# Second MLP projection of a decoder layer: every fourth block of rows by seven half-block products, MLP in three parts

## The chip, the cores and the metric

The kernel runs on one core of a Trainium2 chip. The metric is the device time of one execution in microseconds (us), the median of several runs.

## What is computed

One decoder layer on 256 tokens of width 2048, all in float32: an RMSNorm, one wide projection, three token mixers (a gated MLP over chunks, a state-space model, stick-breaking attention), their gated sum and an output projection, then an MLP, and a last RMSNorm. The change concerns the MLP alone:

```python
h2 = rmsnorm(x, norm2_g[l])
x = x + jnp.square(jax.nn.relu(h2 @ w_mlp_in[l])) @ w_mlp_out[l]   # (256,2048)@(2048,8192), (256,8192)@(8192,2048)
```

The work is nearly all matrix products. Each float32 operand is split into two parts of a reduced float32 type (`F32R`), `hi` = the rounded value and `lo` = the rest, and a product is the sum of three matmuls: hi by hi, lo by hi and hi by lo.

## The kernel before

All weights are read once from HBM in **units** of 128 partitions by 2 x 512 numbers (512 KB). For the second projection (`w_m2`) a unit is 256 rows by 512 columns; for the first (`w_m1`) 512 rows by 256 columns. A list `plan` names the stages with their units in the order of use. `begin_unit(u, lead)` is called as PE's work on unit u is written: it issues SP's DMA up to unit u + 5 (`dma_to`, four buffers `raw`), splits up to unit u + 3 (`conv_to`: ScalarE casts `raw` to `hi`, line 213, then VectorE subtracts to `lo`, line 214; four buffers each), and then, in `flush`, writes whatever is due: work put off by `later(n, f)` to the n-th next unit. So ScalarE and VectorE do their work in the order of these calls: first the split of a unit three ahead, then evacuations and small work that is due. The engines are scheduled by hand in just that order. In the trace VectorE's operations stand under line 86, a helper.

The activations are kept transposed in pairs of 128 x (2 k-tiles, hi and lo, 256 tokens): `xs2` (tile `xz`) for the MLP's input, `ffs[q]` (tile `ff`) for its hidden layer.

- `run_W` (first projection, lines 272 to 296): per unit eight matmuls of 512 columns (line 288) and eight of 256 (line 292) into one tile `mm` of two PSUM banks; four units make 256 hidden columns. One unit later `wide_sum` adds the halves (ScalarE copy at line 301, VectorE addition), and one unit after that `square` applies the squared ReLU and `split2` splits the result into `ffs`.
- `run_N` (second projection, lines 335 to 357): per unit eight matmuls hi by hi and lo by hi (lines 350, 351), then four with `lo` weights (line 353), 12 of 512 columns, into one tile `mm` whose two banks are the two halves of the tokens. After the last unit of a column group the evacuation is due one unit later: VectorE multiplies by the norm's factor and adds to the residual `x2` (`ev_at` in `do_m2`).

The pool `ps_mm` holds two tiles of two banks, taken in turn, and `ps_sd` four tiles of one bank (`side`). `run_W` and `run_N` use one tile of `ps_mm` per group, so that one is filled while the other is read.

The MLP runs in four parts of 2048 hidden columns: eight groups of the first projection (32 units), then four column groups of 512 of the second (32 units, eight per group), which are added to `x2` part by part. The last group of the last part goes through `run_last`, which shortens the kernel's end.

Of the kernel before, what the change touches and what calls it, by code (L numbers as in the profile page):

```python
# [17 lines left out]
P = 128  # L18
# [73 lines left out]
def hybrid_trunk(  # L92
# [36 lines left out]
    def a4(shape, dt, name):  # L129
        return acts.tile(shape, dt, tag="a4", name=name)  # L130
# [10 lines left out]
        return ps_sd.tile([P, 512], F32, tag="sd", name=name)  # L141


    units = []
# [29 lines left out]
    for q in range(4):  # L174
        for i in range(0, 8, 2):
            if (q, i) == (0, 0):
                ab = [add_units(w_m1, 0, 0, 3), add_units(w_m1, 1, 0, 3)]
                for j in range(2):
                    ab[j] += add_units(w_m1, j, 3, 4)
                plan.append(("m1", (q, i), ab))  # L180
            else:
                plan.append(("m1", (q, i), [add_units(w_m1, 8 * q + i + j, 0, 4) for j in range(2)]))
        for i in range(4):
            plan.append(("m2", (q, i), add_units(w_m2, i, 8 * q, 8 * q + 8)))

    raws, loaded = [], {}

    def dma_to(n, parts=1):
        while len(raws) <= min(n, len(units) - 1):
            u = len(raws)  # L190
            raw = wraw.tile([P, 2, 512], F32, tag="raw", name=f"raw{u}")
# [197 lines left out]
    def sumsq(src, acc, junk):  # L389
        S.activation(junk, src, AF.Square, accum_out=acc)  # L390
# [5 lines left out]
    def split2(dst, i, src):  # L396

        t = dst.pair(i)
        S.copy(t[:, :, 0, :], src)
        V.tensor_sub(t[:, :, 1, :], src, t[:, :, 0, :].bitcast(F32))  # L400
# [678 lines left out]

    def do_m1(q, i0, uss):  # L1080
        if i0 == 0:
            ffs[q] = Split(env, 16, f"ff{q}_")

        def ev(ps, i):
            t = wide_sum(ps, f"relu{q}_{i}")

            def square():
                V.scalar_tensor_tensor(out=t, in0=t, scalar=0.0, in1=t, op0=ALU.max, op1=ALU.mult)
                split2(ffs[q], i, t)

            later(1, square)

        groups = [(us, lambda ps, i=i0 + j: ev(ps, i)) for j, us in enumerate(uss)]
        if (q, i0) == (0, 0):
            run_W(groups, xs2)
        else:
            for g in groups:
                run_W([g], xs2)

    def do_m2(q, c, us):  # L1100
        if q == 3 and c == 0:
            for j in range(2):
                f = a4([P, 2, 512], F32, f"fg{j}")
                S.dma_start(f, final_g[j * 1024:(j + 1) * 1024].rearrange("(a c) -> a c", a=2)
                            .partition_broadcast(P))
                fg.extend((f[:, 0, :], f[:, 1, :]))
            fg.append(a4([P, NT, 512], F32, "last"))

        def ev_at(tt, c0, c1, ps):
            v = x2[c][:, tt, c0:c1]  # L1110
            V.scalar_tensor_tensor(out=v, in0=ps, scalar=st2["rsq"][:, tt:tt + 1], in1=v,
                                   op0=ALU.mult, op1=ALU.add)
            if q == 3:
                part = c + (c0 > 0)
                sumsq(v, ss3[:, tt, part:part + 1], ps)
                V.tensor_mul(v if c < 3 else fg[4][:, tt, c0:c1], v, fg[c][:, c0:c1])
                if c == 3 and c1 == 512:
                    finish(tt)

        if (q, c) == (3, 3):  # L1120
            run_last(us, ffs[q], ev_at)
        else:
            run_N(us, ffs[q], lambda tt, ps: ev_at(tt, 0, 512, ps))


    for kind, arg, us in plan:
        if kind == "s5" and arg == 0:
            x_half(0)
            conv_to(0, parts=2)

            def ev0(b, ps):
                V.tensor_mul(s5x[0][:, 2 * b:2 * b + 2, :], ps, rb)

            def mid0(i):
                if i == 0:
                    x_half(1)
                elif i in (1, 3, 5):
                    x_half(i + 1)
                    conv_to(i + 1)
                    x_half(i + 2)  # L1140
                conv_to(max(i + 1, {4: 6, 5: 7, 6: 8, 7: 10}.get(i, 0)))
                if i in (2, 3, 4, 5):
                    load_x(i - 2)
                if i == 6:
                    spawn("rows", norm1_sums())
                if i == 7:
                    s5_load_b()
                    spawn("s5p", s5_prep(), front=False)

            run_T(us, xs, ev0, lead=0, mid=mid0, delay=8)  # L1150
        elif kind in ("s5", "q", "k", "u"):
            do_proj(kind, arg, us)
        elif kind in ("v", "vg"):
            do_nat(kind, arg, us)
        elif kind.startswith("gate"):
            do_gate(int(kind[4]), arg, us)
        elif kind.startswith("br"):
            do_branch(int(kind[2]), arg, us)
        elif kind == "glu":
            do_glu(arg, us)  # L1160
        elif kind == "out":
            do_out(arg, us)
        elif kind == "m1":
            do_m1(*arg, us)
        else:
            do_m2(*arg, us)

# [19 lines left out]
def _layout(x, norm1_g, w_in, b_gate, gm_norm_g, gm_w_s, gm_b_s, s5_lambda_re, s5_lambda_im, s5_log_dt,  # L1187
# [9 lines left out]
    a["w_glu"] = _tiles(s5_w_glu[0])  # L1197
    a["w_m1"] = _tiles_T(w_mlp_in[0])
    a["w_m2"] = _tiles(w_mlp_out[0])
    a["cols"] = np.concatenate([_cols(norm1_g[0]), _cols(norm2_g[0]), _cols(gm_norm_g[0]),  # L1200
                                _cols(s5_d[0]), _cols(s5_b_glu[0])], axis=1)
    a["b_gate"] = b_gate[0]
# [38 lines left out]
```

## Time and profile before

| | |
|---|---|
| time, median of 3 runs (lowest, highest) | 1542.46 us (1542.14, 1542.51) |
| the profiled execution's own time | 1541.8 us |
| its span from first to last instruction | 1540.0 us |
| PE (TensorE) busy | 1529.7 us, 99% |
| VectorE (DVE) busy | 1097.5 us, 71% |
| ScalarE (ACT) busy | 762.7 us, 50% |
| TensorE's mean granted clock | 0.999 |
| moved by DMA | 298.17 MB, mean 194 GB/s |

A matmul's time in the trace holds the way through the array, so neighbours overlap: the distance from one start to the next says what one costs. PEld is the load of the stationary operand, beside PE. What stands in brackets behind a row is how long the engine was idle before it and what ended that.

### The profile page before, as it was taken

Reading aid. Unit: us, or ns where it says so; the run is one execution under the profiler, and the core shown is the slowest. Engines: PE = TensorE matmul, PEld = TensorE weight load, DVE = VectorE, ACT = ScalarE, POOL = GpSimd, SP = SyncE. Lnnn points to the kernel's source line nnn. Section 1 sums busy time; section 2 is a strip of 40 time slices with the busy share of each in tenths; the row PEclk is TensorE's granted clock in tenths of the full one; section 3 lists DMA queues with packets and bytes.
Section 4 is the critical chain, followed back from the end, with each engine's and each line's share of the span. In section 5 each row is a group of like instructions: output and inputs, shape, how many; then the busy total and the mean of one; then the engine's idle time right before and its main releaser. Section 6 shows DMA issues by size and latency. Waiting matters only on the chain.

```text
span 1540.0 us, 20664 instructions
## 1 busy us (share of the span) xinstructions
PE 1529.7 (99%) x7948; PEld 1300.2 (84%) x7948; DVE 1097.5 (71%) x1456; ACT 762.7 (50%) x948; POOL 12.2 (1%) x21
## 2 busy tenths in 40 slices
PE   9999999999999999999999999999999999999997
PEld 9988888888888887898888888888888888888886
DVE  7886978989999999967655665456545655555554
ACT  7446678455555555564454443344433443344442
POOL 0000000000000000000000000000000000000000
PEclk9999999999999999999999999999999999999999
DMA  9654555555555566656666556555555555555653
GB/s 358 200 190 146 188 185 171 185 196 187 189 197 190 193 197 205 191 179 202 209 205 192 191 180 203 192 191 181 198 193 193 181 192 195 195 184 193 217 192 121
DMA packets 85506, 298.17 MB, mean 194 GB/s; under 512 B 9632, under 2 KB 10656, under 8 KB 85408
## 3 DMA queue, kind: packets, MB, share of 16 engines
q1 hardware_dynamic: 79200, 285.25, 55.9%
q10 hardware_dynamic: 6208, 11.61, 2.3%
q8 instruction: 62, 1.02, 0.3%
q14 instruction: 36, 0.29, 0.1%
HBM read 294.73 MB, written 2.10 MB: 193 GB/s over the span
## 4 chain that ended last, share of the span: by engine, by line
PE 96%; DVE 1%; ACT 1%; issue 1%; DMA 0%; POOL 0%; POOLq 0%; DVEq 0%; ACTq 0%
PE mm L288 20%; PE mm L350 20%; PE mm L351 19%; PE mm L353 19%; PE mm L292 10%; PE mm L320 2%; PE mm L319 2%; PE mm L327 1%; PE pb L642 1%; PE py L742 1%; DVE lo L86 0%; PE pwarm L468 0%; DMA raw<-in_w_m 0%; DVE x L86 0%; ACT hi L213 0%
## 5 line engine op out<-in xcount | busy, mean ns | idle before, releaser
L86 DVE TENSOR_TENSOR lo<-raw,hi 128x1024 fp32r<-128x1024 f32 (+1 forms) x537 | 653.7, 1221 | 377.9 <-ACT hi L213 366.1
L213 ACT CAST hi<-raw 128x1024 fp32r<-128x1024 f32 (+1 forms) x537 | 560.6, 1048 | 610.2 <-PE mm L351 377.6
L288 PE MATMUL mm<-xz,hi 128*128 128x512 f32 x1024 | 256.5, 392 | 0.0
L288 PEld LDWEIGHTS mm<-xz,hi 128*128 128x128 f32 x1024 | 184.4, 189 | 33.2
L350 PE MATMUL mm<-hi,xs 128*128 128x512 f32 x512 | 201.4, 393 | 0.0
L351 PE MATMUL mm<-hi,xs 128*128 128x512 f32 x512 | 199.6, 390 | 0.0
L351 PE MATMUL mm<-hi,ff 128*128 128x512 f32 x480 | 186.8, 389 | 0.0
L350 PE MATMUL mm<-hi,ff 128*128 128x512 f32 x480 | 186.8, 389 | 0.0
L292 PEld LDWEIGHTS mm<-xz,lo 128*128 128x128 f32 x1024 | 139.7, 190 | 10.0
L292 PE MATMUL mm<-xz,lo 128*128 128x256 f32 x1024 | 142.8, 282 | 0.0
L353 PE MATMUL mm<-lo,xs 128*128 128x512 f32 x512 | 136.9, 389 | 0.0
L353 PE MATMUL mm<-lo,ff 128*128 128x512 f32 x480 | 128.3, 389 | 0.0
L350 PEld LDWEIGHTS mm<-hi,xs 128*128 128x128 f32 x512 | 96.1, 188 | 23.5 <-issue 4.1
L353 PEld LDWEIGHTS mm<-lo,xs 128*128 128x128 f32 x512 | 96.1, 188 | 20.2
L351 PEld LDWEIGHTS mm<-hi,xs 128*128 128x128 f32 x512 | 96.2, 188 | 19.4
L353 PEld LDWEIGHTS mm<-lo,ff 128*128 128x128 f32 x480 | 90.1, 188 | 18.7
L351 PEld LDWEIGHTS mm<-hi,ff 128*128 128x128 f32 x480 | 90.1, 188 | 18.6
L350 PEld LDWEIGHTS mm<-hi,ff 128*128 128x128 f32 x480 | 90.1, 188 | 18.6
L288 PE MATMUL mm<-xs,hi 128*128 128x512 f32 x384 | 96.9, 394 | 0.0
L288 PEld LDWEIGHTS mm<-xs,hi 128*128 128x128 f32 x384 | 69.1, 189 | 13.6 <-issue 0.7
L86 DVE TENSOR_TENSOR rt<-bu,cs 128x1024 f32<-128x1024 f32 x64 | 76.6, 1220 | 0.3
L292 PEld LDWEIGHTS mm<-xs,lo 128*128 128x128 f32 x384 | 52.4, 190 | 3.8
(247 smaller groups left out, 1619.7 us busy)
## 6 DMA issues: line engine op xcount, KB each, us to landing
raw<-in_w_m SPq DMA_DIRECT2D x256, 512.0 KB, 4.3
raw<-in_w_in SPq DMA_DIRECT2D x143, 512.0 KB, 4.0
raw<-in_w_wide SPq DMA_DIRECT2D x48, 512.0 KB, 3.9
raw<-in_w_br SPq DMA_DIRECT2D x48, 512.0 KB, 4.2
raw<-in_w_out SPq DMA_DIRECT2D x32, 512.0 KB, 3.7
x<-in_x ACTq DMA_DIRECT2D x8, 512.0 KB, 6.1
raw<-in_w_glu SPq DMA_DIRECT2D x8, 512.0 KB, 4.6
gb<-in_b_gate ACTq DMA_DIRECT2D x12, 256.0 KB, 4.3
```

The lines of the kernel that those rows point to most:

```text
L86: return fn(*a, **kw)
L213: S.copy(hi[:, k, :], raw[:, k, :])
L288: PE.matmul(pt[:, nb, :], lhsT=hi[:, k, nb * P:(nb + 1) * P], rhs=src.both(4 * i + k), start=4 * i + k == 0, stop=False)
L292: PE.matmul(pt[:, nb, T:], lhsT=lo[:, k, nb * P:(nb + 1) * P], rhs=src.hi(4 * i + k), start=False, stop=4 * i + k == last)
L319: PE.matmul(po, lhsT=wh, rhs=src.hi(kt), start=kt == 0 and nb % 2 == 0, stop=False)
L320: PE.matmul(po, lhsT=wh, rhs=src.lo(kt), start=False, stop=False)
L327: PE.matmul(po, lhsT=lo[:, k, nb * P:(nb + 1) * P], rhs=src.hi(kt), start=False, stop=kt == 2 * nk - 1 and nb % 2 == 1)
L350: PE.matmul(ps[tt], lhsT=xh, rhs=hi[:, k, :], start=kt == 0, stop=False)
L351: PE.matmul(ps[tt], lhsT=xl, rhs=hi[:, k, :], start=False, stop=False)
L353: PE.matmul(ps[tt], lhsT=xh, rhs=lo[:, k, :], start=False, stop=kt == 2 * nk - 1)
L642: PE.matmul(pbs[h][i][:, ri * T:(ri + 1) * T], lhsT=s5bs[h // 4][r, h % 4, ri * P:(ri + 1) * P], rhs=s5x[h // 4][r, h % 4, :], start=True, ...
L742: PE.matmul(py[h][32 * i:32 * i + 32, :T], lhsT=cks[h][:, ri, i, :], rhs=s[i // 2][:, ri, i % 2, :], start=ri == 0, stop=ri == 1, tile_pos ...
```

## The change

The MLP is cut into three parts of 12, 12 and 8 blocks of 256 hidden columns. In a part, the second projection goes over two halves of 1024 output columns (`do_m2s`, plan kind `m2s`), except for the last half of the last part, which stays two column groups through `run_N` and `run_last`. In a half, every fourth block (k = 0, 4, 8) is done by Strassen's scheme: the block of 256 rows by 1024 columns is two by two half-blocks of 128 by 512, the tokens are two halves, and seven products of three matmuls stand in for eight. There are 3 + 3 + 2 such blocks over the parts for the first half and 3 + 3 for the second, 14 in all. Such a block counts as three units: `a` and `c` come by DMA from `w_seven` (the same numbers as in `w_m2`, in other pairs), `e` is computed from them. The sums of activations (`form`) are made once per block in `do_m1`.

```diff
+PARTS = (12, 12, 8)
+EVERY = 4
...
+        for h in range(2):
+            if (q, h) == (LAST, 1):
+                for c in (2, 3):
+                    plan.append(("m2", (q, c), add_units(w_m2, c, FIRST[q], FIRST[q + 1])))
+                continue
...
+    def split_unit(u, raw):
...
+        S.copy(hi, raw)
+        V.tensor_sub(lo, raw, hi.bitcast(F32))
+        return hi, lo
...
+        if seven[u] == "a":
+            part["a"] = raw
+            loaded[u] = split_unit(u, raw)
+        elif seven[u] == "c":
+            d = part["d"] = s5w.tile([P, 2, 512], F32, tag="T1", name=f"d{u}", bufs=1)
+            part["x"] = raw
+            V.tensor_sub(d, part["a"], raw[:, 0:1, :].to_broadcast([P, 2, 512]))
+            loaded[u] = split_unit(u, d)
+        else:
+            a, d, x = (part.pop(n) for n in "adx")
+            b = s5w.tile([P, 2, 512], F32R, tag="T2", name=f"b{u}", bufs=1)
+            S.copy(b[:, 0, :], x[:, 1, :])
+            V.tensor_sub(b[:, 1, :], x[:, 1, :], b[:, 0, :].bitcast(F32))
+            V.tensor_add(x[:, 0, :], d[:, 1, :], a[:, 0, :])
+            V.tensor_sub(x[:, 1, :], x[:, 1, :], x[:, 0, :])
+            loaded[u] = (*split_unit(u, x), b)
...
+    def run_seven(us, src, forms, evac):
+        top, bot = two_banks(f"top{us[0][0]}"), two_banks(f"bot{us[0][0]}")
+        bank = {(t, c): p[:, c, :] for t, p in enumerate((top, bot)) for c in range(2)}
+        for n in (1, 5, 7, 6):
+            bank[n] = side(f"p{n}_{us[0][0]}")
...
+        def product(b, x, w):
+            mm(b, x[0], w[0])
+            mm(b, x[1], w[0])
+            mm(b, x[0], w[1])
...
+            if len(u) == 3:
+                a = begin_unit(u[0], 3)
+                product(1, half(2 * k, 0), [w[:, 0, :] for w in a])
+                end_unit()
+                d = begin_unit(u[1], 3)
+                product(5, form(k, 0), [w[:, 0, :] for w in d])
+                product(7, form(k, 2), [w[:, 1, :] for w in d])
+                product((0, 1), form(k, 3), [w[:, 1, :] for w in a])
+                end_unit()
+                hi, lo, b = begin_unit(u[2], 3)
+                product((0, 0), half(2 * k + 1, 0), (b[:, 0, :], b[:, 1, :]))
+                product(6, form(k, 1), (hi[:, 0, :], lo[:, 0, :]))
+                product((1, 0), half(2 * k + 1, 1), (hi[:, 1, :], lo[:, 1, :]))
+                if k == shared:
+                    later(1, lambda: evac[0](bank))
+                end_unit()
+            elif k < len(us) - 1:
+                for c in range(2):
+                    w = begin_unit(u[c], 3)
+                    for t in range(NT):
+                        std(u[c], k, c, t, w)
+                    end_unit()
+            else:
+                w0 = begin_unit(u[0], 3)
+                std(u[0], k, 0, 0, w0)
+                end_unit()
+                w1 = begin_unit(u[1], 2)
+                std(u[1], k, 1, 0, w1)
+                std(u[0], k, 0, 1, w0)
+                std(u[1], k, 1, 1, w1)
+                later(1, lambda: evac[1](top, bot))
+                end_unit()
...
+        def ev_shared(bank):
+            p1, p12 = r[0][:, 0, :], r[0][:, 1, :]
+            p21, p22 = r[1][:, 0, :], r[1][:, 1, :]
+            S.copy(p1, bank[1])
+            S.copy(p12, bank[5])
+            V.tensor_add(p21, bank[6], p1)
+            V.tensor_add(p12, p12, p21)
+            V.tensor_add(p22, bank[7], p12)
+            V.tensor_add(p21, bank[7], p21)
+        def ev(top, bot):
+            V.tensor_add(r[0], top, r[0])
+            V.tensor_add(r[1], bot, r[1])
+            for t in range(NT):
+                for c in range(2):
+                    later(1 + t, lambda t=t, c=c: add_m2(q, 2 * h + c, t, 0, 512, r[t][:, c, :]))
```

`std` is the plain product of one unit for one half of the tokens: four matmuls with `hi`, then two with `lo`. The tiles `top` and `bot` are the two tiles of `ps_mm`: the sums of the upper and of the lower half of the tokens for all 1024 columns, filled through the whole half. Four products that go into more than one sum have the four `side` banks (`p`), read by `ev_shared` after the last Strassen block.

Three places of the order on VectorE follow. The first is the **end of a part**, where the second projection ends and the next part's first begins. Before (the evacuation of the last column group is the row `x_3<-mm`):

```order
L86 TENSOR_TENSOR lo_8864<-raw_8825,hi_8863 128x1024
L86 TENSOR_TENSOR lo_8882<-raw_8843,hi_8881 128x1024
L86 TENSOR_TENSOR lo_8901<-raw_8861,hi_8900 128x1024
L86 SCALAR_TENSOR_TENSOR x_3_7337<-mm_8750,rsq,x_3_7337 128x512 x2
L86 TENSOR_TENSOR lo_8925<-raw_8879,hi_8924 128x1024
L86 TENSOR_TENSOR lo_8947<-raw_8898,hi_8946 128x1024
```

Now:

```order
L91 TENSOR_TENSOR lo_9665<-raw_9611,hi_9664 128x1024
L91 TENSOR_TENSOR lo_9669<-raw_9629,hi_9668 128x1024
L91 TENSOR_TENSOR m2r_9185<-top_9187,m2r_9185 128x1024
L91 TENSOR_TENSOR m2r_9186<-bot_9188,m2r_9186 128x1024
L91 TENSOR_TENSOR lo_9693<-raw_9641,hi_9692 128x1024
L91 SCALAR_TENSOR_TENSOR x_2_7164<-m2r_9185,rsq,x_2_7164 128x512
L91 SCALAR_TENSOR_TENSOR x_3_7337<-m2r_9185,rsq,x_3_7337 128x512
```

Behind the splits of the two units that the next stage needs third and fourth stand two additions of 1024 columns, which read `top` and `bot`; the work on `x2` comes later and reads their results. PE's next group there takes the tile of `top`.

The second is the **change of halves** inside a part. Before, at the change from the second column group to the third:

```order
L86 TENSOR_TENSOR lo_8588<-raw_8549,hi_8587 128x1024
L86 TENSOR_TENSOR lo_8607<-raw_8567,hi_8606 128x1024
L86 SCALAR_TENSOR_TENSOR x_1_6991<-mm_8456,rsq,x_1_6991 128x512 x2
L86 TENSOR_TENSOR lo_8627<-raw_8585,hi_8626 128x1024
L86 TENSOR_TENSOR lo_8645<-raw_8604,hi_8644 128x1024
```

Now, from the first half to the second, from the split of unit `a` on:

```order
L91 TENSOR_TENSOR lo_9136<-raw_9099,hi_9135 128x1024
L91 TENSOR_TENSOR d_9153<-raw_9099,raw_9117 128x1024
L91 TENSOR_TENSOR lo_9156<-d_9153,hi_9155 128x1024
L91 TENSOR_TENSOR b_9195<-raw_9117,b_9195 128x512
L91 TENSOR_TENSOR raw_9117<-d_9153,raw_9099 128x512
L91 TENSOR_TENSOR raw_9117<-raw_9117 128x512
L91 TENSOR_TENSOR lo_9201<-raw_9117,hi_9200 128x1024
L91 TENSOR_TENSOR lo_9205<-raw_9151,hi_9204 128x1024
L91 TENSOR_TENSOR m2r_8717<-top_8719,m2r_8717 128x1024
L91 TENSOR_TENSOR m2r_8718<-bot_8720,m2r_8718 128x1024
```

The difference `d`, its split, three half-size steps for `b` and the sums, and the split of `e` now stand ahead of the additions that read `top` and `bot`.

The third is the **start of the first half** of a part, after the last group of the first projection. Before (`relu_7<-mm` evacuates that group):

```order
L86 TENSOR_TENSOR lo_8263<-raw_8209,hi_8262 128x1024
L86 TENSOR_TENSOR lo_8285<-raw_8234,hi_8284 128x1024
L86 TENSOR_TENSOR lo_8308<-raw_8260,hi_8307 128x1024
L86 TENSOR_TENSOR relu_7_8311<-mm_8208,relu_7_8311 128x512
L86 TENSOR_TENSOR lo_8329<-raw_8282,hi_8328 128x1024
L86 SCALAR_TENSOR_TENSOR relu_7_8311<-relu_7_8311 128x512
L86 TENSOR_TENSOR ff_7_8333<-relu_7_8311,ff_7_8333 128x2x256
```

Now, from the split of unit `a` on (`relu_11<-mm` evacuates that group):

```order
L91 TENSOR_TENSOR lo_8643<-raw_8594,hi_8642 128x1024
L91 SCALAR_TENSOR_TENSOR relu_10_8623<-relu_10_8623 128x512
L91 TENSOR_TENSOR ff_10_8647<-relu_10_8623,ff_10_8647 128x2x256
L91 TENSOR_TENSOR d_8668<-raw_8594,raw_8617 128x1024
L91 TENSOR_TENSOR lo_8671<-d_8668,hi_8670 128x1024
L91 TENSOR_TENSOR b_8692<-raw_8617,b_8692 128x512
L91 TENSOR_TENSOR raw_8617<-d_8668,raw_8594 128x512
L91 TENSOR_TENSOR raw_8617<-raw_8617 128x512
L91 TENSOR_TENSOR lo_8698<-raw_8617,hi_8697 128x1024
L91 TENSOR_TENSOR lo_8728<-raw_8666,hi_8727 128x1024
L91 TENSOR_TENSOR relu_11_8731<-mm_8616,relu_11_8731 128x512
```

The addition that reads the last group's tile stands behind the same unit's split as before, but a Strassen block's whole preparation is now ahead of it.

## Rows read from the trace of the kernel before

**Rows 1.** The page: busy time of each engine; the clock TensorE was granted, 40 slices.

```profile
PE 1529.7 (99%) x7948; PEld 1300.2 (84%) x7948; DVE 1097.5 (71%) x1456; ACT 762.7 (50%) x948; POOL 12.2 (1%) x21
...
PEclk9999999999999999999999999999999999999999
```

**Rows 2.** The page: the chain that ended last, shares of the span by line.

```profile
PE mm L288 20%; PE mm L350 20%; PE mm L351 19%; PE mm L353 19%; PE mm L292 10%; PE mm L320 2%; PE mm L319 2%; PE mm L327 1%; PE pb L642 1%; PE py L742 1%; DVE lo L86 0%; PE pwarm L468 0%; DMA raw<-in_w_m 0%; DVE x L86 0%; ACT hi L213 0%
```

**Rows 3.** Timeline, end of the second part: start, us, engine, line, out<-in, [idle before<-releaser].

```profile
1172.61 0.39 PE L350 MATMUL mm<-hi,ff 128*128 128x512 f32 x1
...
1175.33 0.39 PE L350 MATMUL mm<-hi,ff 128*128 128x512 f32 x1
...
1177.14 1.07 PE L353 MATMUL mm<-lo,ff 128*128 128x512 f32 x4
1177.34 1.05 ACT L213 CAST hi<-raw 128x1024 fp32r<-128x1024 f32 x1 [1.67 <-PE mm L351]
...
1178.05 1.98 PE L288 MATMUL mm<-xz,hi 128*128 128x512 f32 x8
1178.42 1.23 DVE L86 TENSOR_TENSOR lo<-raw,hi 128x1024 fp32r<-128x1024 f32 x1 [1.50 <-ACT hi L213]
```

**Rows 4.** Groups of VectorE by shape: line, operation, tiles, shapes, count, busy us, mean ns.

```profile
L86 DVE TENSOR_TENSOR lo<-raw,hi 128x1024 fp32r<-128x1024 f32 x535 | 652.3, 1223 | 377.3 <-ACT hi L213 365.5 <-PE mt L408 6.0 <-PE zt L408 4.5
...
L86 DVE TENSOR_TENSOR ff<-relu,ff 128x512 fp32r<-128x512 f32 x32 | 22.2, 693 | 22.0 <-ACT ff L399 22.0
L86 DVE SCALAR_TENSOR_TENSOR relu<-relu 128x512 f32<-128x512 f32 x32 | 21.9, 685 | 0.0
L86 DVE TENSOR_TENSOR relu<-mm,relu 128x512 f32<-128x512 f32 x32 | 21.9, 684 | 0.0
L86 DVE SCALAR_TENSOR_TENSOR x<-mm,rsq,x 128x512 f32<-128x512 f32 x30 | 21.3, 744 | 0.0
```

**Rows 5.** Groups of ScalarE by shape.

```profile
L213 ACT CAST hi<-raw 128x1024 fp32r<-128x1024 f32 x535 | 559.3, 1050 | 609.7 <-PE mm L351 377.6 <-PE mm L288 119.9 <-issue 71.5
...
L399 ACT CAST ff<-relu 128x512 fp32r<-128x512 f32 x32 | 19.8, 619 | 60.9 <-DVE relu L86 60.9
```

**Rows 6.** Timeline where the second part turns from first to second projection.

```profile
1088.18 2.00 PE L288 MATMUL mm<-xz,hi 128*128 128x512 f32 x8
...
1090.27 1.05 ACT L213 CAST hi<-raw 128x1024 fp32r<-128x1024 f32 x1 [1.75 <-PE mm L288]
...
1090.98 0.40 PE L350 MATMUL mm<-hi,ff 128*128 128x512 f32 x1
...
1091.22 0.58 ACT L301 COPY relu<-mm 128x512 f32<-128x512 f32 x1
1091.35 1.23 DVE L86 TENSOR_TENSOR lo<-raw,hi 128x1024 fp32r<-128x1024 f32 x1 [1.57 <-ACT hi L213]
...
1092.49 0.68 DVE L86 TENSOR_TENSOR relu<-mm,relu 128x512 f32<-128x512 f32 x1
```

**Rows 7.** DMA issues: queue, count, KB each, median us from issue to landing.

```profile
raw<-in_w_m SPq DMA_DIRECT2D x256, 512.0 KB, 4.3
```

**Rows 8.** Windows at the kernel's end: busy time (x instructions), then PEclk, DMA share, GB/s.

```profile
1530.00:1532.00 2.00, 1.69 (x15) 1.49 (x13) 0.27 (x1) 0.00 (x0) 0.00 (x0) 1.00 0.00 0
...
1534.00:1536.00 2.00, 0.00 (x0) 0.00 (x0) 1.29 (x4) 0.00 (x0) 0.00 (x0) 1.00 0.53 196
1536.00:1538.00 2.00, 0.00 (x0) 0.00 (x0) 0.00 (x0) 0.00 (x0) 0.00 (x0) 0.61 0.99 311
```

**Rows 9.** Timeline of PE, first weight unit.

```profile
6.75 0.41 PE L319 MATMUL mm<-xs,hi 128*128 128x256 f32 x1
...
7.18 0.32 PE L319 MATMUL mm<-xs,hi 128*128 128x256 f32 x1
...
7.95 0.28 PE L319 MATMUL mm<-xs,hi 128*128 128x256 f32 x1
...
8.19 0.28 PE L319 MATMUL mm<-xs,hi 128*128 128x256 f32 x1
```

More of the change, by code (lines that the diff above doesn't have):

```diff
@@ L35 @@
 MAGIC = 12582912.0
+PARTS = (12, 12, 8)
+FIRST = [sum(PARTS[:q]) for q in range(len(PARTS) + 1)]
+LAST = len(PARTS) - 1
+EVERY = 4
 C_G1, C_G2, C_GM, C_D, C_GLU = 0, 16, 32, 40, 48
@@ L141, in side @@
         return ps_sd.tile([P, 512], F32, tag="sd", name=name)
-    units = []
+    units, seven = [], {}
     def add_units(src, g, k0, k1):
@@ L173, in hybrid_trunk @@
         plan.append(("out", i, add_units(w_out, i, 0, 8)))
-    for q in range(4):
-        for i in range(0, 8, 2):
+    for q, nk in enumerate(PARTS):
+        for i in range(0, nk, 2):
+            g = FIRST[q] + i
             if (q, i) == (0, 0):
@@ L181, in hybrid_trunk @@
             else:
-                plan.append(("m1", (q, i), [add_units(w_m1, 8 * q + i + j, 0, 4) for j in range(2)]))
-        for i in range(4):
-            plan.append(("m2", (q, i), add_units(w_m2, i, 8 * q, 8 * q + 8)))
+                plan.append(("m1", (q, i), [add_units(w_m1, g + j, 0, 4) for j in range(2)]))
+        for h in range(2):
[3 more added lines that the diff above has]
+                continue
+            us = []
+            for k in range(nk):
+                ku = FIRST[q] + k
+                if k % EVERY == 0:
+                    n = len(units)
+                    units.extend((w_seven[h, ku // EVERY, 0], w_seven[h, ku // EVERY, 1], None))
+                    seven.update({n: "a", n + 1: "c", n + 2: "e"})
+                    us.append((n, n + 1, n + 2))
+                else:
+                    us.append([add_units(w_m2, 2 * h + c, ku, ku + 1)[0] for c in range(2)])
+            plan.append(("m2s", (q, h), us))
     raws, loaded = [], {}
@@ L190, in dma_to @@
             u = len(raws)
+            if units[u] is None:
+                raws.append(None)
+                continue
             raw = wraw.tile([P, 2, 512], F32, tag="raw", name=f"raw{u}")
@@ L204, in conv_to @@
             raws[u] = None
+            if u in seven:
+                conv_seven(u, raw)
+                nconv[0] += 1
+                continue
             if u >= len(units) - 4:
@@ L216, in conv_to, with conv_seven @@
             nconv[0] += 1
+    part = {}
+    def split_unit(u, raw):
+        hi = whi.tile([P, 2, 512], F32R, tag="hi", name=f"hi{u}")
+        lo = wlo.tile([P, 2, 512], F32R, tag="lo", name=f"lo{u}")
+        S.copy(hi, raw)
+        V.tensor_sub(lo, raw, hi.bitcast(F32))
+        return hi, lo
+    def conv_seven(u, raw):
+        if seven[u] == "a":
[14 more added lines that the diff above has]
+            loaded[u] = (*split_unit(u, x), b)
     BAR = "bar"
@@ L358, in run_N, with mm, half, form @@
             end_unit()
+    def run_seven(us, src, forms, evac):
[3 more added lines that the diff above has]
+            bank[n] = side(f"p{n}_{us[0][0]}")
+        triples = sum(len(u) == 3 for u in us)
+        left = {b: 6 * (len(us) - triples) for b in bank if b not in (1, 5, 6, 7)}
+        for b in (1, 5, 6, 7, (0, 0), (0, 1), (1, 0)):
+            left[b] = left.get(b, 0) + 3 * triples
+        begun = set()
+        def mm(b, x, w):
+            left[b] -= 1
+            PE.matmul(bank[b], lhsT=x, rhs=w, start=b not in begun, stop=left[b] == 0)
+            begun.add(b)
+        def half(kt, t):
+            return tuple(x[:, t * P:(t + 1) * P] for x in (src.hi(kt), src.lo(kt)))
+        def form(k, f):
+            return tuple(forms[k][:, f, e, :] for e in range(2))
+        def product(b, x, w):
+            mm(b, x[0], w[0])
+            mm(b, x[1], w[0])
+            mm(b, x[0], w[1])
+        def std(u, k, c, t, w):
+            for part in range(2):
+                for e in range(2):
+                    xh, xl = half(2 * k + e, t)
+                    if part == 0:
+                        mm((t, c), xh, w[0][:, e, :])
+                        mm((t, c), xl, w[0][:, e, :])
+                    else:
+                        mm((t, c), xh, w[1][:, e, :])
+        shared = max(k for k, u in enumerate(us) if len(u) == 3)
+        for k, u in enumerate(us):
+            if len(u) == 3:
[20 more added lines that the diff above has]
+                    end_unit()
+            else:
+                w0 = begin_unit(u[0], 3)
[7 more added lines that the diff above has]
+                end_unit()
+        assert not any(left.values())
@@ L1089, in square, with sums @@
                 split2(ffs[q], i, t)
+                if i % EVERY == 0:
+                    later(1, sums)
+            def sums():
+                f = s5w.tile([P, 4, P], F32, tag="gb", name=f"sums{q}_{i}", bufs=1)
+                V.scalar_tensor_tensor(out=f[:, 0, :], in0=t[:, 0, P:], scalar=-1.0, in1=t[:, 1, P:],
+                                       op0=ALU.mult, op1=ALU.subtract)
+                V.scalar_tensor_tensor(out=f[:, 1, :], in0=f[:, 0, :], scalar=-1.0, in1=t[:, 0, :P],
+                                       op0=ALU.mult, op1=ALU.subtract)
+                V.tensor_sub(f[:, 2, :], t[:, 0, :P], t[:, 0, P:])
+                V.tensor_sub(f[:, 3, :], t[:, 1, :P], f[:, 1, :])
+                fs = forms[q][i] = a4([P, 4, 2, P], F32R, f"form{q}_{i}")
+                S.copy(fs[:, :, 0, :], f)
+                V.tensor_sub(fs[:, :, 1, :], f, fs[:, :, 0, :].bitcast(F32))
             later(1, square)
@@ L1098, in do_m1, with load_fg @@
                 run_W([g], xs2)
-    def do_m2(q, c, us):
[L1101 to L1121, printed above, removed]
-        else:
-            run_N(us, ffs[q], lambda tt, ps: ev_at(tt, 0, 512, ps))
+    def load_fg():
+        for j in range(2):
+            f = a4([P, 2, 512], F32, f"fg{j}")
+            S.dma_start(f, final_g[j * 1024:(j + 1) * 1024].rearrange("(a c) -> a c", a=2)
+                        .partition_broadcast(P))
+            fg.extend((f[:, 0, :], f[:, 1, :]))
+        fg.append(a4([P, NT, 512], F32, "last"))
@@ new lines, in add_m2 @@
+    def add_m2(q, c, tt, c0, c1, ps):
+        v = x2[c][:, tt, c0:c1]
+        V.scalar_tensor_tensor(out=v, in0=ps, scalar=st2["rsq"][:, tt:tt + 1], in1=v,
+                               op0=ALU.mult, op1=ALU.add)
+        if q == LAST:
+            n = c + (c0 > 0)
+            sumsq(v, ss3[:, tt, n:n + 1], ps)
+            V.tensor_mul(v if c < 3 else fg[4][:, tt, c0:c1], v, fg[c][:, c0:c1])
+            if c == 3 and c1 == 512:
+                finish(tt)
+    def do_m2(q, c, us):
+        if c == 3:
+            run_last(us, ffs[q], lambda tt, c0, c1, ps: add_m2(q, c, tt, c0, c1, ps))
+        else:
+            run_N(us, ffs[q], lambda tt, ps: add_m2(q, c, tt, 0, 512, ps))
@@ new lines, in do_m2s @@
+    def do_m2s(q, h, us):
+        if q == LAST:
+            load_fg()
+        r = [a4([P, 2, 512], F32, f"m2r{q}{h}{t}") for t in range(NT)]
+        def ev_shared(bank):
[13 more added lines that the diff above has]
+                    later(1 + t, lambda t=t, c=c: add_m2(q, 2 * h + c, t, 0, 512, r[t][:, c, :]))
+        run_seven(us, ffs[q], forms[q], (ev_shared, ev))
@@ L1164, in hybrid_trunk @@
             do_m1(*arg, us)
+        elif kind == "m2s":
+            do_m2s(*arg, us)
         else:
@@ L1199, in _layout @@
     a["w_m2"] = _tiles(w_mlp_out[0])
+    b = a["w_m2"].reshape(2, 2, -1, P, 2, 512)[:, :, ::EVERY]
+    a["w_seven"] = np.stack([np.stack([b[:, r, :, :, 0], b[:, 1 - r, :, :, 1]], axis=3) for r in range(2)],
+                            axis=2)
     a["cols"] = np.concatenate([_cols(norm1_g[0]), _cols(norm2_g[0]), _cols(gm_norm_g[0]),
```

6 lines of the change are left out of this document (4 added, 2 removed).

## Prediction

> **What bounds the kernel now.** I read the page's busy times first: PE is busy 99% of the span, at a granted clock of 9 tenths or more in all 40 slices [rows 1]. The chain that ended last says the same of the path: its large shares are all matmul lines, and VectorE's and ScalarE's lines have 0% each [rows 2]. So a matmul removed is time gained, and a wait put on PE is time lost, one for one. VectorE (71%) and ScalarE (50%) have room on average.
>
> The price of a matmul is read from the timeline: two units of the second projection start 2.72 us apart, at 1172.61 and 1175.33 [rows 3], and hold 12 matmuls of 512 columns, so one costs 2.72 / 12 = 0.227 us. A unit of the first projection takes 1090.98 - 1088.18 = 2.80 us [rows 6].
>
> The same timelines show how stages follow each other now. At the end of a part the next matmul starts at 1178.05, one matmul's distance behind the last [rows 3]; where the first projection turns into the second PE goes on at 1090.98 while the tile just filled is emptied by ScalarE at 1091.22 and by VectorE at 1092.49 [rows 6]. PE waits at neither, since it goes on in the other tile of its pool. These places are what the change alters.
>
> **The change part by part.** *Matmuls.* A Strassen block needs 7 x 3 = 21 matmuls where two units need 24. With 14 blocks, 42 matmuls go: 42 x 0.227 = **9.5 us gained**. Order of the sums, fewer parts and the doubled width add or remove none.
>
> *Work on VectorE and ScalarE.* Per block VectorE has four steps of 1024 columns (the splits of a, c and e, and d) at 1.22 us and three of 512 at 0.69 [rows 4]: 7.0 us, where two units have 2.4. PE needs 21 x 0.227 = 4.8 us for the block, so VectorE falls behind inside it, but four blocks of rows together cost VectorE 7.0 + 6 x 1.22 = 14.3 us against 4.8 + 6 x 2.72 = 21.1 us of PE. With splits three units ahead I cost this at nothing inside a half; its cover is the plain units ahead of the block, whose splits take half of their time. The sums in `do_m1` (four steps of 128 columns, each under the 0.69 of 512, one of 512, and a cast of 0.62 [rows 5]) fit into a group of 4 x 2.80 = 11.2 us, in which VectorE has 4 x 1.22 + 3 x 0.69 = 7.0. The two DMAs of a block carry the same 512 KB each as two units' did. A raw buffer is held a little longer, and one DMA takes 4.3 us to land [rows 7], which lies within the three units' lead: nothing.
>
> *New waits.* `run_seven` takes both tiles of `ps_mm` and fills them to the end of a half. So whatever comes next has no free tile, and PE waits for VectorE where it did not. There are eight such places. I work each out with t = 0 where PE would start the next stage, and with three habits of the rows: a matmul ends 0.39 us after its start; a cast starts 0.04 us after the end of the last matmul that reads the old `hi` (which started one matmul before 1177.14, so it ended at 1177.30, and the cast starts at 1177.34); a subtraction starts 0.03 us after its cast [rows 3].
>
> (1) *End of a part, into the next part's first group, and in the last part into its third column group: three times.* The last unit's `hi` is read up to the third matmul from the end: it starts at -0.68 and ends at -0.29. The cast that takes this buffer runs from -0.25 to 0.80 (1.05 us [rows 5]), its subtraction from 0.82 to 2.05, and only then the addition that empties `top`. It has 1024 columns and no row of its own. From below, a subtraction of 1024 from the other memory takes 1.22; from above, two additions of 512 out of PSUM take 2 x 0.68 = 1.37 [rows 4]. I take 1.22, since for 512 columns the two memories differ by 0.01. So `top` is free at 3.25 and PE starts at about **3.3 us**. At best the addition goes ahead of one split (2.1); at worst PE needs `bot` too, one addition later (4.5).
>
> (2) *First half to second half, twice.* PE has nine matmuls in the `side` banks first, 9 x 0.227 = 2.04 us, then needs `top`. VectorE's queue up to `top` is the block's whole preparation: from the cast of a (its buffer is read until -8.45, three units ahead) cast 1.05, split 1.22, d 1.22, cast 1.05, split 1.22, three half steps 2.07, cast 1.05, split 1.22, the next unit's split 1.22, addition 1.22. That is 12.5 us and 0.2 of gaps from -8.42: `top` is free at 4.25, a wait of **2.2 us**. If the preparation were no bound, the splits at the end would still give some 3.0 - 2.04, 1.0; if it is later by a DMA or a cast, 3.5.
>
> (3) *First projection to first half, three times.* `top` is long free; `bot` holds the last group of the first projection and is needed after 18 matmuls, at 4.08. The queue starts with the cast of a at -9.09, three units of 2.80 and the 0.71 us by which a cast leads a unit [rows 6]: cast 1.05, split 1.22, the group's square 0.69, cast 0.62, subtraction 0.69, then as in (2) from d to the next unit's split 9.05, and the addition that empties `bot`, 0.68. The sum is 14.0 us, so `bot` is free at 4.9. The wait is **0.9 us**, between 0 and 2.
>
> *Sum.* Waits 3 x 3.3 + 2 x 2.2 + 3 x 0.9 = 17.0 us (8 to 26 with the ends above), gain 9.5: the profiled execution goes from 1541.8 to 1549.3. The median of the runs lies 0.66 above that execution, so I forecast **1550.0 us**, 7.5 us or 0.5% slower, and 1541 to 1559 with the bounds.
>
> *The clock.* In the windows of the kernel's end PE's last matmul is over at 1531.7, the granted clock is still 1.00 until 1536 and 0.61 from there to 1538 [rows 8]; with levels of 2.4 and 1.2 GHz, 0.61 is 0.44 us at the upper and the rest at the lower, so the fall came after some 4.7 us of rest. My longest wait is 3.3, so I let the clock stay. The Trainium skill's page "TensorE: Matmul & The Clock Gate", section "HAM oscillation", warns of just such waits between bursts of matmuls, after each of which the array is back at half its clock; the rows of the end bear out the fall, but after a longer rest, and by it the sum would be that of the second rival.
>
> **The rivals.** *The banks come free in time* (faster). If VectorE reads each tile before PE needs it, only the 42 matmuls are left: 1542.5 - 9.5 = 1533.0. It decides where the eight waits sum to under 9.5 - 3.1 = 6.4 us, under 0.8 each. For it: VectorE idles much of the second projection [rows 1, 4], and today's changes of stage cost PE nothing [rows 3, 6]. Against: the additions can't start before the last matmul of a half, two splits stand ahead of them, and no third tile exists. Chance 0.08.
>
> *The clock falls at the long waits* (slower still). The first weight unit shows what that costs: two matmuls of 256 columns take 7.18 - 6.75 = 0.43 us early and 8.19 - 7.95 = 0.24 soon after [rows 9]. PE's work had begun at about 1 us, so some 6 us at half pace lose about 3 us. One to three falls give 1553 to 1559. For it: three waits over 3 us. Against: the rows of the end, 4.7 us. Chance 0.12.
>
> *Only the ends of parts cost.* If the block's preparation runs ahead, the five waits of (2) and (3) fall under 0.5 us each: 9.9 + 2.5 - 9.5 = 2.9 at most and 0.4 at least, so 1543 to 1545. What counts is whether d and the half steps are done before the half ends; they wait for no matmul, but for the split of a, which does. Chance 0.13.
>
> *VectorE becomes the bound at each block*: if the lead is used up, each of 14 blocks loses up to 7.0 - 4.8 = 2.2 us, 31 in all; half of that gives 1565. Against: 14.3 of 21.1 us. Chance 0.04.
>
> *The change doesn't do what it says*: the order on PE has 42 fewer matmuls of 512 columns, so I leave that out.
>
> **How the numbers follow.** The forecast has 0.63. Its own bounds reach 1541 to 1559, most of it 1545 to 1555. The range that holds eight in ten leaves out the fast rival, the blocks as a bound, and two or three falls of the clock: 1542 to 1557. A measurement of this kernel can tell 0.2%, 3.1 us, from no change. Faster by more than that: the fast rival and a tail of the third, 0.09. Within it (1539.4 to 1545.5): most of the third rival and the forecast's low end, 0.15. Slower: the rest, 0.76.
>
> **What would show it.** Right: PE's waits on the addition that reads `top`, at three ends of parts, near 3 us each, and on `top` near 2 us at two changes of halves; 42 fewer matmuls at an unchanged 0.227; the clock at 1.00. The first column of the waits would name `m2r` as what `mm` and `top` waited for. Wrong: no PE waits of over 1 us in the MLP (the fast rival), a clock under 1.00 in slices of the MLP (the second), or waits on `hi` and `lo` inside the halves (the fourth).

## The result: 15.8 us slower, where 7.5 were forecast

The changed kernel took 1558.26 us (1557.83 to 1560.14) against 1542.45: a ratio of 1.0105, 95% interval 1.0088 to 1.0123. Slower was right, the size was not: the time lies 1.3 us above the range. The profiled execution took 1557.83 us.

The page of the changed kernel, busy times and granted clock, answers to [rows 1]:

```profile
PE 1529.2 (98%) x7906; PEld 1295.7 (83%) x7906; DVE 1183.3 (76%) x1588; ACT 790.8 (51%) x994; POOL 12.2 (1%) x21
...
PEclk9999999999999999999999999999999999999999
```

PE is busy as long as before, though 42 matmuls fewer stand in the span, which is 16 us longer. The clock's digits are 9 as before, since slices of 39 us average over what follows; its mean over the span is 0.993 where it was 0.999. The list of PE's waits, those in the MLP (us in total, times, longest), where before had none ([rows 3, 6] show two of the places):

```profile
PE mm L345 <- DVE m2r L91: 6.3, 2, 3.2
PE top L433 <- DVE m2r L91: 4.0, 2, 2.0
PE mm L407 <- DVE m2r L91: 3.2, 1, 3.2
PE bot L433 <- DVE relu L91: 1.8, 3, 0.6
```

These are the eight places of the forecast: three ends of parts (2 + 1), two changes of halves, three starts of a first half. The timeline of the first end of a part, where the second projection ran into the first without a wait before [rows 3]:

```profile
1090.84 2.58 DVE L91 TENSOR_TENSOR lo<-raw,hi 128x1024 fp32r<-128x1024 f32 x2 [2.86 <-ACT hi L241]
1090.91 0.61 PE L433 MATMUL bot<-lo,ff 128*128 128x512 f32 x2
...
1093.33 1.22 DVE L91 TENSOR_TENSOR m2r<-top,m2r 128x1024 f32<-128x1024 f32 x1
1094.47 1.22 DVE L91 TENSOR_TENSOR m2r<-bot,m2r 128x1024 f32<-128x1024 f32 x1
...
1094.70 3.75 PE L345 MATMUL mm<-xz,hi 128*128 128x512 f32 x8 [3.17 <-DVE m2r L91]
...
1098.25 1.91 PE L349 MATMUL mm<-xz,lo 128*128 128x256 f32 x8
...
1099.95 2.20 PE L345 MATMUL mm<-xz,hi 128*128 128x512 f32 x8
...
1102.94 1.32 PE L345 MATMUL mm<-xz,hi 128*128 128x512 f32 x5
```

The queue is the one worked out: two splits end at 1093.42, the addition that empties `top` runs behind them, and PE starts 0.15 us after it. From the last start before (1090.91 and one matmul, 1091.14) to 1094.70 are 3.56 us, 3.3 more than a matmul's 0.227. But then the next group's unit takes 1099.95 - 1094.70 = 5.25 us, where it took 2.80 [rows 6], and the one behind it 1102.94 - 1099.95 = 2.99. The windows (busy times, then the granted clock) say why:

```profile
1092.00:1094.00 2.00, 0.00 (x0) 0.00 (x0) 1.88 (x3) 0.16 (x1) 0.00 (x0) 0.88 0.46 117
1094.00:1096.00 2.00, 1.30 (x3) 1.14 (x4) 1.68 (x2) 0.00 (x0) 0.00 (x0) 0.50 0.84 266
...
1098.00:1100.00 2.00, 2.00 (x11) 1.90 (x10) 0.00 (x0) 1.04 (x1) 0.00 (x0) 0.50 0.00 0
1100.00:1102.00 2.00, 2.00 (x10) 1.61 (x10) 1.75 (x2) 0.00 (x0) 0.00 (x0) 0.92 0.00 0
```

The clock fell inside PE's rest, at about 1093.5 (0.88 over 2 us is 0.48 us at half of the full clock), and came back at about 1100.3 (0.92). The third end of a part shows the same:

```profile
1500.64 0.77 PE L407 MATMUL mm<-hi,ff 128*128 128x512 f32 x1 [3.17 <-DVE m2r L91]
...
1508.95 0.39 PE L407 MATMUL mm<-hi,ff 128*128 128x512 f32 x1
```

Two units, 24 matmuls, lie between these starts: 8.31 us where 2 x 2.72 = 5.44 are the rule.

The timeline of the first change of halves:

```profile
1025.98 0.39 PE L433 MATMUL p<-lo,form 128*128 128x512 f32 x1
...
1027.02 1.22 DVE L91 TENSOR_TENSOR m2r<-top,m2r 128x1024 f32<-128x1024 f32 x1
...
1028.38 0.94 PE L433 MATMUL top<-hi,form 128*128 128x512 f32 x2 [2.01 <-DVE m2r L91]
...
1032.80 1.08 PE L433 MATMUL top<-hi,ff 128*128 128x512 f32 x4
```

and the windows there, with a shorter fall:

```profile
1026.00:1028.00 2.00, 0.37 (x2) 0.00 (x0) 2.00 (x2) 1.04 (x1) 0.00 (x0) 1.00 0.53 131
1028.00:1030.00 2.00, 1.62 (x5) 1.30 (x6) 2.00 (x3) 0.64 (x1) 0.00 (x0) 0.66 0.90 279
1030.00:1032.00 2.00, 2.00 (x6) 1.61 (x5) 2.00 (x4) 0.41 (x1) 0.00 (x0) 0.50 0.56 199
1032.00:1034.00 2.00, 2.00 (x10) 1.57 (x10) 2.00 (x3) 1.05 (x1) 0.00 (x0) 0.98 0.51 195
```

Here PE rested from 1026.4 to 1028.38, and the clock fell after PE had begun again, at about 1028.6, for some 3.4 us: the first 12 matmuls took 1032.80 - 1028.38 = 4.42 us where 2.72 are the rule. The second change of halves has a rest of the same 2.01 us, and the second end of a part one of 3.17, and neither is followed by a fall. Behind the second change the 12 matmuls take 1302.80 - 1299.94 = 2.86 us with the clock at 1.00, and the rows of that end show a unit at nearly its usual pace, 1367.56 - 1364.70 = 2.86 us:

```profile
1364.70 2.06 PE L345 MATMUL mm<-xz,hi 128*128 128x512 f32 x8 [3.17 <-DVE m2r L91]
...
1367.56 1.78 PE L345 MATMUL mm<-xz,hi 128*128 128x512 f32 x7
```

The timeline at the start of a first half, with the third kind of wait:

```profile
963.77 0.39 PE L433 MATMUL p<-lo,form 128*128 128x512 f32 x1
964.01 0.68 DVE L91 TENSOR_TENSOR relu<-mm,relu 128x512 f32<-128x512 f32 x1
...
964.75 0.74 PE L433 MATMUL bot<-hi,ff 128*128 128x512 f32 x2 [0.59 <-DVE relu L91]
```

The group of the new additions out of PSUM (count, ns min/median/max):

```profile
L91 DVE TENSOR_TENSOR m2r<-top,m2r x5: 1215/1217/1218, 1027.0 to 1499.3; 128x1024 f32<-128x1024 f32 x5
```

The addition of 1024 columns takes 1.217 us; I had taken 1.22 between 1.22 and 1.37.

### The profile page after: what moved, and what is told of

It is laid out like the page before. It is cut to its first block, busy times and chain, and to the rows that moved or that the text cites. A ratio compares the mean times of both kernels' runs of the same rounds, so it can differ in the third digit from the quotient of the medians.

```text
span 1556.1 us, 20790 instructions
## 1 busy us (share of the span) xinstructions
PE 1529.2 (98%) x7906; PEld 1295.7 (83%) x7906; DVE 1183.3 (76%) x1588; ACT 790.8 (51%) x994; POOL 12.2 (1%) x21
## 5 line engine op out<-in xcount | busy, mean ns | idle before, releaser
L241 ACT CAST hi<-raw 128x1024 fp32r<-128x1024 f32 (+1 forms) x509 | 530.0, 1049 | 486.6 <-PE mm L408 216.0
L349 PEld LDWEIGHTS mm<-xz,lo 128*128 128x128 f32 x1024 | 140.5, 191 | 10.1
L433 PE MATMUL bot<-hi,ff 128*128 128x512 f32 x364 | 98.9, 390 | 1.8 <-DVE relu L91 1.8
L433 PE MATMUL top<-hi,ff 128*128 128x512 f32 x336 | 89.9, 389 | 0.0
L433 PEld LDWEIGHTS bot<-hi,ff 128*128 128x128 f32 x364 | 68.2, 188 | 17.3 <-DVE relu L91 3.1
L433 PEld LDWEIGHTS top<-hi,ff 128*128 128x128 f32 x336 | 63.1, 188 | 13.3
L251 ACT CAST hi<-raw 128x1024 fp32r<-128x1024 f32 x28 | 29.5, 1052 | 60.0 <-DVE raw L91 38.9
L433 PE MATMUL bot<-lo,ff 128*128 128x512 f32 x182 | 57.2, 389 | 0.0
```

Source lines behind the costliest of these rows:

```text
L251: S.copy(hi, raw)
L349: PE.matmul(pt[:, nb, T:], lhsT=lo[:, k, nb * P:(nb + 1) * P], rhs=src.hi(4 * i + k), start=False, stop=4 * i + k == last)
L433: PE.matmul(bank[b], lhsT=x, rhs=w, start=b not in begun, stop=left[b] == 0)
```

## The experiments

All are edits of the changed kernel. Two theories stood after the result: **(T)** the eight waits as forecast, and on top some 8 us of matmuls at half the clock, which the waits bring about; **(R)** the remainder is work that the change adds or delays (VectorE's load, the new form of matmul, the longer parts).

**e_fill: PE kept busy in the waits.** The fills write a bank that no one reads afterwards.

```diff
+        def fill(po, n):
+            for i in range(n):
+                PE.matmul(po, lhsT=src.hi(0)[:, 0:P], rhs=src.both(0), start=True, stop=True)
...
+                if k == 0:
+                    fill(bank[6], fills[0])
                 product((0, 1), form(k, 3), [w[:, 1, :] for w in a])
...
+        if fills[2]:
+            fill(side(f"fill{us[0][0]}"), fills[2])
...
```

> The changed kernel with matmuls of no use put where PE waits: nine before the first product into top at each change of halves, three before product 6 at the start of a first half, fourteen at each end of a part; each 512 columns, 0.227 us, into a bank that is not read afterwards. They fit into the waits measured in the changed kernel (starts 2.40, 0.98 and 3.57 us apart where 0.227 is the rule, so 2.2, 0.75 and 3.3 us), so by themselves they move nothing. Theory (some 8 us of the change's cost are matmuls at half the clock after the waits): PE has no rest, the granted clock stays at 1.00 to the last matmul, and the time falls from 1558.3 to about 1550. Rival (the remainder is something else, such as slower matmuls in the new form or work of VectorE that is late): the time stays at 1558, or rises by what the fills overrun.

Measured: 1551.04 us, ratio to before 1.0057 (1.0040 to 1.0074). The windows around the first end of a part:

```profile
1090.00:1092.00 2.00, 2.00 (x10) 1.67 (x9) 1.87 (x3) 0.55 (x1) 0.00 (x0) 1.00 0.29 66
1092.00:1094.00 2.00, 1.99 (x9) 1.37 (x8) 2.00 (x2) 0.00 (x0) 0.00 (x0) 1.00 0.84 270
1094.00:1096.00 2.00, 2.00 (x15) 1.78 (x14) 0.08 (x1) 0.78 (x1) 0.00 (x0) 1.00 0.50 193
```

With the waits still there, but no rest, the clock stays at 1.00 (0.999 over the span, as before the change) and 7.2 us come back by the medians, 6.7 between the profiled executions. That is the price of the falls, and it is not VectorE's: its work is the same (1184.2 us busy against 1183.3). 1.7 us above 1542.2 - 9.5 + 16.6 are left: 0.6 lie ahead of the MLP, whose first matmul starts at 824.88 instead of 824.31, and 1.1 inside the halves, where e_early_relu has them too.

**e_early: the waits taken away where both tiles are read too late.** `top` is complete 2.7 us before `bot`; it is now read then.

```diff
                 std(u[1], k, 1, 0, w1)
+                evac[1](0, top)
                 std(u[0], k, 0, 1, w0)
+                conv_to(u[1] + 3)
                 std(u[1], k, 1, 1, w1)
-                later(1, lambda: evac[1](top, bot))
+                evac[1](1, bot)
...
```

> The changed kernel, but top is read as soon as its last matmul is written, ahead of the next unit's split, while PE still fills bot for 2.7 us; bot is read ahead of the last split. Theory (PE waits for the tiles of ps_mm alone): the waits at three ends of parts go from 3.3 us to none, at two changes of halves from 2.2 to about 0.3, at three starts of a first half they stay at 0.75; the clock stays at 1.00. 1542.5 - 9.5 + 0.6 + 2.3 = 1535.9 us. Rival (VectorE's load is the bound and the waits only show it): waits of the same sum turn up at the splits of the block that is prepared at the change of halves, and the time stays over 1545.

Measured: 1536.47 us, ratio 0.9962 (0.9947 to 0.9977). In the list of PE's waits one group of the MLP is left:

```profile
PE bot L433 <- DVE relu L91: 1.8, 3, 0.6
```

Five waits go, and the clock's mean is back at 0.999. VectorE is busy as long as before, 1183.6 us, so its load was not behind them. What turns up elsewhere is small, and the forecast had it (0.3 at each change of halves): the next block there waits for the addition that reads `bot`, as the next run's rows show.

**e_early_relu: the third kind of wait too.** In the first unit of a half what is due is written ahead of the split.

```diff
+        if due_first:
+            flush()
         conv_to(u + lead)
...
+                a = begin_unit(u[0], 3, due_first=k == 0)
```

> As e_early, and at the start of a first half the last group of the first projection is read ahead of the split of the unit three ahead. Theory: the three waits of 0.75 us go too, since that addition then ends at about 3.8 us and PE needs the tile at 4.1: 1533.6 us, all of the 42 matmuls' 9.5 us but 0.6. Rival: the split that now comes later is what PE waits for next, 0.5 us or more each, and the time is that of e_early.

Measured: 1533.96 us, ratio 0.9946 (0.9931 to 0.9961), faster than both kernels. PE's waits of the whole profile, none in the MLP:

```profile
PE pwarm L605 <- POOL ones L588: 1.0, 1, 1.0
PE pyc L999 <- ACT le L991: 0.9, 1, 0.9
```

Against the 1532.7 that 42 matmuls alone would give, 1.3 us are missing. Most of them lie inside the halves. The first two take 1086.23 - 959.24 = 126.99 us; at the same place e_parts, with plain units alone, has 576 matmuls in 1090.42 - 959.83 = 130.59, so 18 fewer would take 126.5. The same reckoning gives 0.5 for the second pair of halves and 0.1 for the last half: 1.1 us in all. About 0.5 of it is a wait that the list of PE's waits leaves out, since the load of the weights has it:

```profile
1026.86 0.30 PEld L435 LDWEIGHTS bot<-hi,ff 128*128 128x128 f32 x2 [0.40 <-DVE m2r L91]
```

It delays PE by 0.24 us at each of the two changes of halves. The other 0.6 are spread over the 14 blocks, some 0.04 us in each; their cause is open. So (R) has a small share: 1.1 us, and it stays with the waits taken away.

**e_parts: the cut into parts alone** (second projection by `run_N` in all parts, no halves, no Strassen blocks):

```diff
-            if (q, h) == (LAST, 1):
-                for c in (2, 3):
+            if True:
+                for c in (2 * h, 2 * h + 1):
                     plan.append(("m2", (q, c), add_units(w_m2, c, FIRST[q], FIRST[q + 1])))
...
-                if i % EVERY == 0:
-                    later(1, sums)
```

> Three parts of 12, 12 and 8 blocks alone: the second projection stays in column groups of 512 through run_N, with no half of 1024 columns, no sums and no Strassen block. Theory: the cut into parts costs and gives nothing, since the tiles of ps_mm still alternate: 1542.5 us within 0.5. Rival (a longer part, with twelve pairs of ff alive, makes something wait, or one change of stage less gives something): off by over 1 us.

Measured: 1542.22 against 1542.18, ratio 1.0000 (0.9991 to 1.0009). The parts cost nothing, as costed.

**e_ends and e_halves: which rest lets the clock fall.** The early read at the ends of parts alone, and at the changes of halves alone. The last line is that of e_ends; e_halves has `not (h == 1 or q == LAST)` there:

```diff
...
+                if early:
+                    evac[1](1, bot, 1)
+                else:
+                    later(1, lambda: evac[1](0, top, 0))
+                    later(1, lambda: evac[1](1, bot, 0))
...
+        run_seven(us, ffs[q], forms[q], (ev_shared, ev), h == 1 or q == LAST)
```

> The early read of top and bot (as in e_early) at the three ends of parts alone; the two changes of halves and the three starts of a first half stay as in the changed kernel, with rests of 2.2 and 0.75 us. Theory (each rest costs its own length, and a fall of the clock if the rest is long enough): 1542.2 - 9.5 + 2 x 2.2 + 3 x 0.75 = 1539.3 us, and if rests of 2.2 us let the clock fall as one of the two did in the changed kernel's profile, 1.7 us more for each, up to 1543. Rival (only rests of over 3 us let it fall, and the one at the change of halves came from something before it): 1539.3 and a clock of 1.00.

Measured: 1542.23 us, ratio 0.9998 (0.9988 to 1.0007). Each change of halves is followed by a fall:

```profile
1026.00:1028.00 2.00, 0.02 (x1) 0.00 (x0) 2.00 (x3) 0.93 (x1) 0.00 (x0) 1.00 0.58 193
1028.00:1030.00 2.00, 1.96 (x6) 1.57 (x7) 2.00 (x2) 1.05 (x1) 0.00 (x0) 0.63 0.89 264
...
1292.00:1294.00 2.00, 0.46 (x2) 0.45 (x3) 2.00 (x3) 0.42 (x1) 0.00 (x0) 1.00 0.83 274
1294.00:1296.00 2.00, 2.00 (x8) 1.59 (x7) 2.00 (x3) 1.05 (x1) 0.00 (x0) 0.69 0.75 248
```

1539.3 and two times 1.7 are 1542.7. The rival falls: rests of 2.0 us can be enough. They aren't always: of ten executions, one took 1540.76 us at a mean clock of 0.998, the others 1541.92 to 1543.44 at 0.996 or 0.997, so it seems to have had one fall fewer (an estimate from these means; it has no trace).

> The early read at the two changes of halves alone; the three ends of parts keep their rests of 3.3 us, the starts of a first half theirs of 0.75. Without any fall: 1542.2 - 9.5 + 3 x 3.35 + 2 x 0.3 + 3 x 0.75 = 1545.6 us. Theory (a rest of 3.3 us lets the clock fall in most cases, 2.8 us lost each, as at two of three ends in the changed kernel's profile): 1551 with two falls, 1554 with three. Rival (the falls need the two rests that lie closer together): 1545.6.

Measured: 1552.62 us, ratio 1.0065 (1.0050 to 1.0080): 7.0 above the 1545.6 without falls, so 2.3 us for each of three falls where 2.8 had been expected. Each end of a part is followed by one, among them the second, which went without in the changed kernel's profile:

```profile
1088.00:1090.00 2.00, 0.00 (x0) 0.00 (x0) 1.88 (x3) 0.41 (x1) 0.00 (x0) 1.00 0.29 63
1090.00:1092.00 2.00, 1.05 (x3) 0.89 (x4) 1.93 (x2) 0.00 (x0) 0.00 (x0) 0.62 0.89 297
...
1356.00:1358.00 2.00, 0.32 (x1) 0.35 (x2) 2.00 (x3) 0.00 (x0) 0.00 (x0) 0.68 0.93 281
...
1494.00:1496.00 2.00, 0.00 (x0) 0.00 (x0) 2.00 (x2) 0.00 (x0) 0.00 (x0) 1.00 0.66 201
1496.00:1498.00 2.00, 1.68 (x5) 1.39 (x6) 1.30 (x2) 0.00 (x0) 0.00 (x0) 0.67 0.85 272
```

Whether a given rest brings a fall is thus not fixed by its length alone; what else decides was not tried.

**e_every2: every second block by the seven products**, on e_early_relu:

```diff
-EVERY = 4
+EVERY = 2
```

> As e_early_relu, but every second block instead of every fourth by the seven products: 28 blocks, 84 matmuls fewer, 19.05 us. Theory that PE stays the bound: 1542.2 - 19.05 + 0.6 = 1523.8 us. Rival that VectorE becomes it: a block and a plain pair cost VectorE 7.0 + 2.4 = 9.4 us against 4.8 + 5.4 = 10.2 of PE, and a half of six such pairs has 8 us more of evacuations, so 64.6 against 61.2 us: up to 3.4 us lost in each of five halves, less what the lead of three units takes up, 1527 to 1541 us, with PE's waits on lo and hi inside the halves.

Measured: 1603.52 us, ratio 1.0397 (1.0381 to 1.0412). Both expectations missed, the rival's by 62 us, though PE waits for `lo` and `hi` inside the halves as it said. The page's busy times:

```profile
PE 1539.9 (96%) x7864; PEld 1282.3 (80%) x7864; DVE 1254.1 (78%) x1698; ACT 812.7 (51%) x1030; POOL 12.2 (1%) x21
```

and the largest of PE's waits in the MLP:

```profile
PE p L435 <- DVE lo L91: 18.1, 35, 0.5
PE p L435 <- ACT hi L251: 15.1, 29, 1.9
PE mm L347 <- DVE m2r L91: 6.5, 2, 3.3
```

VectorE is busy only 78% of the span, ScalarE 51%, and yet PE waits for both in 64 places at the blocks. VectorE's rows from one block's `d` to the next one's:

```profile
994.28 1.22 DVE L91 TENSOR_TENSOR d<-raw,raw 128x1024 f32<-128x1024 f32 x1
996.69 1.23 DVE L91 TENSOR_TENSOR lo<-d,hi 128x1024 fp32r<-128x1024 f32 x1 [1.19 <-ACT hi L251]
...
1001.04 4.63 DVE L91 TENSOR_TENSOR lo<-raw,hi 128x1024 fp32r<-128x1024 f32 x4 [1.19 <-ACT hi L251]
1005.74 1.23 DVE L91 TENSOR_TENSOR d<-raw,raw 128x1024 f32<-128x1024 f32 x1
```

From `d` to `d` are 11.46 us, where a block and a plain pair take PE 10.2. VectorE works for 9.1 of them, near the 9.4 that I had priced, and stands still twice for 1.19, while ScalarE casts what VectorE has just computed. The preparation is one chain through two engines (cast, split, d, cast, split, three half steps, cast, split: 10.1 us by the durations of [rows 4, 5]), and a second one is due every 10.2 us with the plain units' splits in between; the sum per engine, from which I priced it, leaves out that each engine stands still while the other works. This is read from the trace and not tested. Another part may be the DMAs: the chain that ended last has 2.8% of the span, 45 us, in those of `w_seven`, into buffers that the preparation holds until its sums are made. PE's waits in the MLP sum to 48.5 us, and the mean granted clock is 0.993; the distance to 1523.8 is 79.7. How it divides between the chain, restarts, the clock and late DMAs was not settled.

## Why the prediction was wrong

*Matmuls: right.* 42 went at an unchanged 0.227 us, 9.5 us; with PE's listed waits removed 8.2 us of it are seen (e_early_relu), and 1.1 us of the rest lie in the halves.

*The waits: right.* Forecast 3.3, 2.2 and 0.9; measured from start to start, less one matmul, 3.3, 2.2 and 0.75 (1094.70 - 1091.14, 1028.38 - 1025.98 and 964.75 - 963.77, each less 0.23). Sum 16.6 us against 17.0, and e_early and e_early_relu take away what they should. The queue behind each was as worked out. (The terms of the third wait, 4.9 - 4.08, give 0.8 and not 0.9.)

*The other work at nothing: right to about 1 us at every fourth block* (e_early_relu, e_parts), and only there (e_every2).

*The clock: wrong, and the step that failed.* "My longest wait is 3.3, so I let the clock stay." It rested on the kernel's end before [rows 8], where the clock fell 4.7 us after the last matmul. I read that one case as a length of rest that is needed, when it is only one that sufficed. In the changed kernel the clock fell 2.0 us after the last matmul at one place and at another when PE had already resumed after a rest of 2.0 us. The price of a fall had been worked out nearly right in the second rival, at about 3 us. The three falls cost 2.6 us (two units in 8.24 us for 5.60, first end of a part), 1.7 (first change of halves) and 2.9 (last end of a part), 7.2 in all, which is what e_fill gives back. So 1541.8 - 9.5 + 16.6 + 7.2 = 1556.1 for the profiled execution, against 1557.83. Of the other 1.7 us, 0.6 lie before the MLP, whose first matmul starts at 824.93 instead of 824.31: PE waits twice for ScalarE's casts in the first 11 us (0.93 and 0.41 us), which it does neither before nor in e_early_relu. The other 1.1 us lie inside the halves, as in e_early_relu. The rival's chance was 0.12. The range was meant to leave out two or three falls; by the rival's price it held two (1556) and left out only three (1559). That three falls came, as many as the rival's waits of over 3 us, is chance: one of these three waits brought none, and one fall came at a change of halves, where the rest was 2.0 us and the rival expected none.

The Trainium skill's page "TensorE: Matmul & The Clock Gate", section "HAM oscillation", tells of a kernel whose matmuls wait some 3 to 5 us for DMA between bursts, each of which then starts at the lower clock. These runs agree that such waits bring the clock down, at 1.7 to 2.9 us for each fall, and differ in two points: rests of 2.0 us were enough, and not every rest brought a fall.

## What to carry to other kernels

Where a stage fills every buffer of a pool, the next stage's first matmul waits for the last read of the oldest one; read each buffer when its last matmul is written, ahead of any conversion that merely prepares later work (here 22 us between the two orders of the same instructions, some 7 of them the clock's). A wait of 2 us or more on TensorE is to be priced at its own length and, with a good chance (8 of the 10 such rests below), a spell at half the clock on top; where it can't be removed, matmuls of no use in its place gave back some 7 us here. When extra work is laid on helper engines, cost the longest chain through them within the time of one step too, not only each engine's sum.

## What was not expected of the hardware

The clock can fall after a rest is over: at a change of halves PE resumed at 1028.38 and the clock went to 0.50 at about 1028.6, and in e_ends PE resumed at 1293.54 and the fall came in the window from 1294 to 1296 (0.69 there, so at about 1294.8). Rests of the same 2.01 us were followed by a fall three times out of four (the changed kernel's profile and e_ends), and rests of 3.17 us five times out of six (the changed kernel's and e_halves').
